# A rotation of 96 images by 90 degrees: the first group loaded in 8 KB rows and turned by way of PSUM, 1 MB of the last group stored in half rows

## The chip, the core and the metric

The kernel runs on one core of a Trainium2 chip. The metric is the device time of one execution in microseconds (us), lower is better; the time before is the median of three runs. Beside these, one execution was taken by the hardware profiler: its span (from the first to the last profiled instruction) and its own time are a little apart, and both are given below. The engines that matter here are VectorE (DVE in the profile), ScalarE (ACT), SyncE (SP), which issues all transfers, and the sixteen DMA engines that carry them between the device memory (HBM) and the on-chip memory (SBUF).

## The reference

```
x: (32, 3, 256, 256) float32
return np.rot90(x, k=-1, axes=(-2, -1)).astype(np.float32)
```

Every one of the 96 images of 256 x 256 is turned clockwise by a quarter: a transposition of each image, with the order of the new columns reversed. Nothing is computed; 25.17 MB are read and 25.17 MB are written.

## The kernel before

All 96 x 256 image rows are taken as one long list. A **slab** is 128 x 16 of them (2 MB): on each of the 128 partitions lie 16 rows of 256 floats, 16 KB. Four groups, u0 to u3, hold 2, 2, 4 and 4 slabs (4, 4, 8 and 8 MB, `sizes` at L38), all of them at once in SBUF, each with a buffer of its own. Two half-slab buffers `spare[0]` and `spare[1]` lie in PSUM, and `extra` and `most` in SBUF.

**Transfers.** SyncE issues every transfer, in the order of the program: first the loads of u0, u1, u2, u3 (L54 to L59), then the stores of u0 to u3 (L154 to L158). A load covers every second partition of u0 or u1 (64 partitions, rows of 16 KB) or every fourth of u2 or u3 (rows of 32 KB), 2 MB each; the very first and the very last load are cut into two of 1 MB. A store covers every second partition (64) with all slabs of the group, in rows of 16 KB: 2 MB for u0 and u1, 4 MB for u2 and u3, two stores a group (a = 0 and 1). The first store has a dependency by hand on `mark`, the first of the last two loads (L160), so that no store runs ahead of the loads. The transfers use eight semaphores in turn, so that a transfer also waits for the landing of the one eight places before it.

**The turn.** VectorE's transpose instruction turns blocks of 32 x 32; the rest of the rotation is done by the access patterns of its input (`src`, L83) and output (`dst`, L85), which permute positions inside a partition and reverse them. A group is turned in place. For this it is cut into quarters: by the halves of the input's column index c (low, high) and of its row index r, called A, B, C, D (L108). A quarter of a pair of slabs is 128 x 2048 elements. A quarter may overwrite only what has been read already, so one quarter first *leaves* into a spare buffer (L88, a VectorE turn into `spare` or `most`), the others *move* in place (L97), and the first *enters* by copies on ScalarE (L93). In u2 and u3, which have four slabs, some quarters are instead copied to a line buffer by ScalarE (`line`, L100), turned there by VectorE, and copied back (`unline`, L104).

**The order of the work.** `keep` (L63) chains all instructions of VectorE, and all of ScalarE, in the order in which they stand in the program. So the order around the change is written out by hand (L115 to L152): u0 leaves to `spare[0]`, moves D, C, B, and enters on ScalarE; u1 the same by way of `spare[1]`; then u2, whose first copy (`line` A into `extra`, L122) stands on ScalarE's queue ahead of the two copies that enter u1 (L124); then `line` D into `spare[1]` (L127); then the moves of u2. Of u3, a quarter of two slabs is first copied to `spare[1]` (`kept`, L136), a quarter leaves to `most` and a piece of `spare[0]`, six moves run (D, C, B, for each of two pairs of slabs), ScalarE's copies enter what left, and the last VectorE instruction turns `kept` into the last quarter (L152). That last turn writes the lower half of every 16 KB row of u3, and so do the copies before it; the upper halves are written by the moves of C and B.

Of the kernel before, what the change touches and what calls it, by code (L numbers as in the profile page):

```python
# [1 line left out]

# [4 lines left out]


@with_exitstack
def kernel(  # L10
    ctx: ExitStack,
    tc: tile.TileContext,
    x: bass.AP,
    out: bass.AP,
):

    nc = tc.nc
    fp32 = mybir.dt.float32

    B, C, H, W = x.shape
    P = nc.NUM_PARTITIONS
    R = 16
    E = R * W  # L30
    Q = E // 2
    hw = R // 2
    low, high = slice(0, hw), slice(hw, R)

    rows_in = x.rearrange("b c h w -> (b c h) w")
    rows_out = out.rearrange("b c h w -> (b c h) w")

    sizes = (2, 2, 4, 4)  # L38
    first = [sum(sizes[:n]) for n in range(len(sizes))]
    groups = [  # L40
        ctx.enter_context(tc.tile_pool(name=f"group{n}", bufs=1)).tile([P, s, E], fp32, name=f"u{n}")
        for n, s in enumerate(sizes)
    ]
    psum = ctx.enter_context(tc.tile_pool(name="psum", bufs=1, space=bass.MemoryType.PSUM))
    spare = [psum.tile([P, Q], fp32, name=f"spare{h}") for h in range(2)]
    extra = ctx.enter_context(tc.tile_pool(name="extra", bufs=1)).tile([P, Q], fp32, name="extra")
    cut = hw - 1
    most = ctx.enter_context(tc.tile_pool(name="most", bufs=1)).tile([P, Q // hw * cut], fp32, name="most")

    for n, I in enumerate(sizes):  # L50
        ld = rows_in[first[n] * P * R : (first[n] + I) * P * R]
        ld = ld.rearrange("(a i m r) w -> i m a (r w)", a=2, i=I, m=P // I)
        to = groups[n].rearrange("p s f -> p (s f)").rearrange("p (a f) -> p a f", a=2)
        for i in range(I):  # L54
            if (n, i) in ((0, 0), (len(sizes) - 1, I - 1)):
                mark = nc.sync.dma_start(out=to[i::I, 0], in_=ld[i][:, 0])  # L56
                nc.sync.dma_start(out=to[i::I, 1], in_=ld[i][:, 1])  # L57
            else:
                nc.sync.dma_start(out=to[i::I], in_=ld[i])  # L59

    last = {}

    def keep(inst):  # L63

        before = last.get(inst.ins.engine)
        if before is not None:
            tc.add_manual_dep(inst.ins, before, mybir.DependencyInfo(
                mybir.DependencyClass.NoSync, mybir.DependencyReason.SCHED_ONLY), reason="order")
        last[inst.ins.engine] = inst.ins.name

    def turn(out, in_):
        keep(nc.vector.transpose(out=out, in_=in_))  # L72

    def copy(out, in_):
        keep(nc.scalar.copy(out=out, in_=in_))  # L75

    class Group:
        def __init__(self, n):
            I = sizes[n]
            self.I, self.T = I, I // 2  # L80
            self.K = W // (R * self.T)
            u = groups[n].rearrange("p s f -> p (s f)")
            self.src = u.rearrange("p (a t r g c) -> p t c r g a", a=2, t=self.T, r=R, c=R)  # L83
            self.raw = u.rearrange("p (a t r g c) -> p t a r g c", a=2, t=self.T, r=R, c=R)
            self.dst = u.rearrange("p (i c k t r) -> p t c r k i", i=I, c=R, k=self.K, t=self.T)[:, ::-1, :, ::-1, ::-1, :]  # L85
            self.back = u.rearrange("p (i c k t r) -> p t i c k r", i=I, c=R, k=self.K, t=self.T)[:, ::-1]

        def leave(self, t, held, c=low, n=hw):  # L88

            kept = held.rearrange("p (i c k r) -> p c r k i", i=self.I, c=n, k=self.K)  # L90
            turn(out=kept[:, :, ::-1, ::-1, :], in_=self.src[:, t, c, low])

        def enter(self, t, held, i, c=low, n=hw):  # L93
            kept = held.rearrange("p (i c k r) -> p i c k r", i=self.I, c=n, k=self.K)
            copy(out=self.back[:, t, i, c, :, high], in_=kept[:, i])

        def move(self, t, c, r):  # L97
            turn(out=self.dst[:, t, c, r], in_=self.src[:, t, c, r])

        def line(self, t, c, r, row):  # L100
            row = row.rearrange("p (c r g a) -> p c r g a", c=hw, r=hw, a=2)
            copy(out=row, in_=self.src[:, t, c, r])

        def unline(self, t, c, r, row):  # L104
            row = row.rearrange("p (c r k i) -> p c r k i", c=hw, r=hw, k=self.K)
            copy(out=self.dst[:, t, c, r], in_=row)

    A, B_, C_, D = (low, low), (high, low), (high, high), (low, high)  # L108

    def turn_pair(g, held):  # L110
        g.leave(0, held)
        for q in (D, C_, B_):
            g.move(0, *q)

    g0, g1, g2, g3 = [Group(n) for n in range(4)]  # L115
    turn_pair(g0, spare[0])
    for i in range(2):
        g0.enter(0, spare[0], i)
    turn_pair(g1, spare[1])


    g2.line(0, *A, extra)  # L122
    g2.leave(1, spare[0])
    for i in range(2):  # L124
        g1.enter(0, spare[1], i)
    turn(out=extra, in_=extra)
    g2.line(0, *D, spare[1])  # L127
    g2.move(1, *D)
    turn(out=spare[1], in_=spare[1])
    g2.unline(0, *D, spare[1])  # L130
    for q in (C_, B_):
        for t in range(2):
            g2.move(t, *q)


    kept = spare[1].rearrange("p (a r g c) -> p a r g c", a=2, r=hw, c=hw)  # L136
    for a in range(2):
        copy(out=kept[:, a], in_=g3.raw[:, 0, a, low, :, low])
    for i in (0, 2, 1, 3):
        g2.enter(1, spare[0], i)  # L140
    rest = spare[0][:, : Q // hw]
    g3.leave(1, most, slice(0, cut), cut)
    g3.leave(1, rest, slice(cut, hw), 1)
    g2.unline(0, *A, extra)
    for q in (D, C_, B_):
        for t in range(2):
            g3.move(t, *q)
    for i in (0, 2, 1, 3):
        g3.enter(1, most, i, slice(0, cut), cut)
    held = rest.rearrange("p (i k r) -> p i k r", i=4, k=g3.K)  # L150
    copy(out=g3.back[:, 1, :, cut, :, high], in_=held)
    turn(out=g3.dst[:, 0, low, low], in_=kept.rearrange("p a r g c -> p c r g a"))  # L152

    for n, I in enumerate(sizes):  # L154
        st = rows_out[first[n] * P * R : (first[n] + I) * P * R]
        st = st.rearrange("(a i m r) w -> a m i (r w)", a=2, i=I, m=P // 2)
        for a in range(2):
            put = nc.sync.dma_start(out=st[a], in_=groups[n][a::2])  # L158
            if (n, a) == (0, 0):
                tc.add_manual_dep(put.ins, mark.ins.name, mybir.DependencyInfo(  # L160
                    mybir.DependencyClass.Sync, mybir.DependencyReason.SCHED_ONLY), reason="stores after loads")


# [1 line left out]
_INS = ['x']  # L165
_OUTS = [((32, 3, 256, 256), 'float32')]


# [23 lines left out]
```

## Time and profile before

| what | us |
|---|---|
| time, median of three runs (123.68 to 123.89) | 123.74 |
| the profiled execution's own time | 123.72 |
| its span | 121.9 |
| VectorE busy | 85.6 (25 turns) |
| ScalarE busy | 27.3 (20 instructions) |
| SyncE's queue: share of the sixteen DMA engines' span | 97.0% |
| first turn of u0 starts | 13.39 |
| first turn of u1 starts | 27.85 |
| first turn of u2 starts | 42.55 |
| first store issued | 59.61 |
| last turn ends | 99.52 |

The page gives the busy time of each engine, then the span in 40 equal slices with the busy share of a slice in tenths (9 is 90% or more), with the mean share of the DMA engines in the same slices; then the chain that ended last, and groups of instructions. In a line of a group or of the timeline stand the line of the kernel, the engine, the operation, output <- input by the program's names without buffer numbers (all four groups are `u` there), and what ended the engine's idle time before it. SPq is SyncE's queue, with the time that it spent on issuing a transfer, not the time of the transfer itself. Besides these views the trace holds, for each DMA packet, its start and length, and the moment of each landing.

### The profile page before, as it was taken

How to read it: one execution, taken by the hardware profiler on the slowest of the kernel's cores; microseconds unless marked ns; L12 is line 12 of the kernel's file. 1: busy time of each engine (PE TensorE's matmuls, PEld its weight loads, DVE VectorE, ACT ScalarE, POOL GpSimd, SP SyncE). 2: the span in 40 equal slices, each digit the busy share in tenths (PEclk: the TensorE clock that was granted, in tenths of full speed). 3: DMA queues.
4: the chain of work that ended last, by engine and by line, in shares of the span. 5: the costliest groups of instructions: out<-in, count | busy, mean ns of one | idle time of the engine just before them, and what ended most of it. 6: DMA issues, size and time to landing. Idle time of an engine off the chain costs nothing.

```text
span 121.9 us, 132 instructions
## 1 busy us (share of the span) xinstructions
DVE 85.6 (70%) x25; ACT 27.3 (22%) x20; POOL 0.2 (0%) x4
## 2 busy tenths in 40 slices
DVE  0000699999999999999999999999999960000000
ACT  0000400006000099928363194000003400000000
POOL 0000000000000000000000000000000000000000
DMA  3999999998979897979899999999999989999994
GB/s 86 387 430 435 441 435 435 446 505 355 516 344 516 344 516 344 516 344 516 344 430 430 430 430 430 425 425 430 430 430 430 430 355 430 430 430 430 430 430 172
DMA packets 2912, 50.33 MB, mean 413 GB/s; under 512 B 352, under 2 KB 352, under 8 KB 352
## 3 DMA queue, kind: packets, MB, share of 16 engines
q1 hardware_dynamic: 2912, 50.33, 97.0%
HBM read 25.17 MB, written 25.17 MB: 413 GB/s over the span
## 4 chain that ended last, share of the span: by engine, by line
DVE 44%; DMA 30%; SPq 4%; issue 3%; DVEq 0%
DVE u L72 33%; DMA u<-in_x_dram 30%; DVE spare L72 6%; SPq L59 3%; DVE most L72 3%; DVE extra L72 2%; SPq L56 0%; SPq L57 0%; DVEq L72 0%
## 5 line engine op out<-in xcount | busy, mean ns | idle before, releaser
L72 DVE STREAM_TRANSPOSE u<-u 128x2048 f32<-128x2048 f32 x17 | 62.6, 3734 | 0.3
L72 DVE STREAM_TRANSPOSE spare<-u 128x2048 f32<-128x2048 f32 (+1 forms) x4 | 11.9, 2979 | 13.6 <-DMA u<-in_x_dram 13.6
L75 ACT COPY u<-spare 128x1024 f32<-128x1024 f32 (+3 forms) x10 | 10.2, 1062 | 20.7 <-DVE u L72 18.0
L75 ACT COPY extra<-u 128x2048 f32<-128x2048 f32 x1 | 4.2, 4235 | 12.6 <-DMA u<-in_x_dram 12.6
L75 ACT COPY spare<-u 128x1024 f32<-128x1024 f32 (+1 forms) x3 | 6.0, 2016 | 2.9 <-DMA u<-in_x_dram 2.9
L75 ACT COPY u<-most 128x448 f32<-128x448 f32 x4 | 2.1, 564 | 20.3 <-DVE u L72 20.3
L75 ACT ACT_TABLE_LOAD x1 | 1.3, 1283 | 13.3 <-DMA u<-in_x_dram 13.3
L75 ACT COPY u<-extra 128x2048 f32<-128x2048 f32 x1 | 3.7, 3739 | 0.0
L72 DVE STREAM_TRANSPOSE u<-spare 128x2048 f32<-128x2048 f32 x1 | 3.6, 3605 | 0.0
L72 DVE STREAM_TRANSPOSE most<-u 128x1792 f32<-128x1792 f32 x1 | 3.6, 3603 | 0.0
L72 DVE STREAM_TRANSPOSE spare<-spare 128x2048 f32<-128x2048 f32 x1 | 2.5, 2474 | 0.0
L72 DVE STREAM_TRANSPOSE extra<-extra 128x2048 f32<-128x2048 f32 x1 | 2.3, 2311 | 0.0
L176 POOL MEMSET const-bfloat16-1.0<- 128x1 bf16 x1 | 0.1, 102 | 0.0
L176 POOL MEMSET const-uint8-127<- 128x1 uint8 x1 | 0.1, 102 | 0.0
L176 POOL MEMSET const-float32-1.0<- 128x1 f32 x1 | 0.1, 99 | 0.0
L176 POOL MEMSET const-float32-0.0<- 128x1 f32 x1 | 0.1, 98 | 0.2 <-issue 0.2
## 6 DMA issues: line engine op xcount, KB each, us to landing
u<-in_x_dram SPq DMA_DIRECT2D x10, 2048.0 KB, 30.2
out_dram<-u SPq DMA_DIRECT2D x4, 4096.0 KB, 18.7
out_dram<-u SPq DMA_DIRECT2D x4, 2048.0 KB, 13.4
u<-in_x_dram SPq DMA_DIRECT2D x4, 1024.0 KB, 20.5
```

What stands on the lines that cost most here:

```text
L59: nc.sync.dma_start(out=to[i::I], in_=ld[i])
L72: keep(nc.vector.transpose(out=out, in_=in_))
L75: keep(nc.scalar.copy(out=out, in_=in_))
L176: nc = _bacc.Bacc("TRN2", target_bir_lowering=False, num_devices=1)
```

## The change

For u0 the layout, the loads, the turn and the place in the program are new. A slab's 128 partitions now hold two runs of 8 rows from two places 1 MB apart, in rows of 8 KB. The second slab's rows come first, as two loads of 1 MB over all 128 partitions, then the first slab's as one load of 2 MB. The first slab buffer is turned by two VectorE instructions into `spare[0]` and `spare[1]`, the second one by two instructions into the first slab buffer, and ScalarE copies both spares into the second slab buffer in two copies of 128x2048. So the quarters, with `leave`, `move` and `enter`, are gone for u0; the number of VectorE instructions is the same. u1 leaves to `extra` instead of `spare[1]`, and it enters before u2's first copy and not after it. The stores of u0 keep their size and their 16 KB rows.

At the end, the store of the even partitions of u3 (a = 0, 4 MB) becomes three: the upper halves of slab 0's rows (64 x 8 KB, 512 KB), the lower halves (512 KB), and the other three slabs (3 MB). The a = 1 store stays whole.

```diff
-    for n, I in enumerate(sizes):
-        ld = rows_in[first[n] * P * R : (first[n] + I) * P * R]
-        ld = ld.rearrange("(a i m r) w -> i m a (r w)", a=2, i=I, m=P // I)
+    def rows_of(rows, n):
+        return rows[first[n] * P * R : (first[n] + sizes[n]) * P * R]
+    ld = rows_of(rows_in, 0).rearrange("(s i p r) w -> s i p (r w)", s=2, i=2, p=P)
+    home = [groups[0][:, s].rearrange("p (i f) -> p i f", i=2) for s in range(2)]
+    for i in range(2):
+        nc.sync.dma_start(out=home[0][:, i], in_=ld[1, i])
+    nc.sync.dma_start(out=home[1], in_=ld[0].transpose([1, 0, 2]))
+    for n in range(1, len(sizes)):
...
-    g0, g1, g2, g3 = [Group(n) for n in range(4)]
-    turn_pair(g0, spare[0])
+    def turn_slab(src, dsts):
+        s = src.rearrange("p (i r g c) -> p c r g i", i=2, r=R // 2, c=R)
+        for h, d in enumerate(dsts):
+            d = d.rearrange("p (c k r) -> p c r k", c=hw, r=R // 2)[:, :, ::-1, ::-1]
+            turn(out=d, in_=s[:, h * hw : (h + 1) * hw])
+    u = groups[0]
+    turn_slab(u[:, 0], spare)
+    turn_slab(u[:, 1], [u[:, 0, :Q], u[:, 0, Q:]])
+    for h in range(2):
+        copy(out=u[:, 1, h * Q : (h + 1) * Q], in_=spare[h])
+    g1, g2, g3 = [Group(n) for n in range(1, 4)]
+    turn_pair(g1, extra)
     for i in range(2):
-        g0.enter(0, spare[0], i)
-    turn_pair(g1, spare[1])
+        g1.enter(0, extra, i)
     g2.line(0, *A, extra)
     g2.leave(1, spare[0])
-    for i in range(2):
-        g1.enter(0, spare[1], i)
...
+    for n in range(1, len(sizes)):
+        I = sizes[n]
+        st = rows_of(rows_out, n).rearrange("(a i m r) w -> a m i (r w)", a=2, i=I, m=P // 2)
         for a in range(2):
-            put = nc.sync.dma_start(out=st[a], in_=groups[n][a::2])
+            done = 0
+            if (n, a) == (len(sizes) - 1, 0):
+                done = 1
+                for f in (slice(Q, E), slice(0, Q)):
+                    nc.sync.dma_start(out=st[a][:, 0, f], in_=groups[n][a::2, 0, f])
+            nc.sync.dma_start(out=st[a][:, done:], in_=groups[n][a::2, done:])
```

## The prediction

> **What bounds the kernel now.** I read the page's slices first, because they show how full the transfers are; then SyncE's own waits, since one queue issues every transfer; then the instructions in order of time around each border of the stages; last the transfer records, for the holes.
>
> The span and the slices of the page:
>
> ```profile
> span 121.9 us, 132 instructions
> ...
> DVE  0000699999999999999999999999999960000000
> ACT  0000400006000099928363194000003400000000
> ...
> DMA  3999999998979897979899999999999989999994
> ...
> DMA packets 2912, 50.33 MB, mean 413 GB/s; under 512 B 352, under 2 KB 352, under 8 KB 352
> ```
>
> The DMA row is at 9 nearly from end to end, while VectorE is idle in the first tenth and the last sixth. So the time is the start (first packet at 2.1 us), 50.33 MB at the engines' pace, whatever holes there are, and the end. The page's 97.0% for the queue leaves 3% of 121.9, about 3.7 us: 2.1 before the first packet, 1.3 after the last one at 120.65, and a remainder of some tenths.
>
> Where is the remainder? Windows of the trace (duration, then DVE, ACT and POOL busy, clock, DMA share, GB/s):
>
> ```profile
> 97.00:104.00 7.00, 2.52 (x1) 0.22 (x1) 0.00 (x0) 1.00 0.93 391
> 104.00:119.00 15.00, 0.00 (x0) 0.00 (x0) 0.00 (x0) 1.00 1.01 431
> ```
>
> A share of 0.93 over 7 us is 0.49 us missing. The transfer records place it: the sixteen engines run out between 100.29 and 100.74 and start again between 100.86 and 101.00, on average 0.44 us idle each. The instructions of that stretch say why:
>
> ```profile
> 92.17 1.04 ACT L75 COPY u<-most 128x448 f32<-128x448 f32 x2 [17.63 <-DVE u L72]
> 95.92 1.03 ACT L75 COPY u<-most 128x448 f32<-128x448 f32 x2 [2.71 <-DVE u L72]
> 95.92 3.60 DVE L72 STREAM_TRANSPOSE u<-spare 128x2048 f32<-128x2048 f32 x1
> 96.85 0.36 ACT L75 COPY u<-spare 128x256 f32<-128x256 f32 x1
> 99.60 1.26 SPq L158 DMA_DIRECT2D out_dram<-u  x2
> ```
>
> The last turn ends at 99.52, the stores of u3 are issued from 99.60, and their first packets come 1.27 us after that, at 100.87, when group 2's stores are already through. SyncE's waits from 95 us on confirm it:
>
> ```profile
> SPq L158 <- DVE u L72: 22.9, 1, 22.9
> SPq L187 <- DMA out_dram<-u: 20.1, 3, 10.2
> ```
>
> The two stores of u3 (4 MB each) land 10.19 and 9.74 us after what was before them; the 0.45 between is the hole. **So two things can change the time: how long the packets take, and that hole of 0.44 us.** VectorE matters through the hole alone.
>
> **Part 1: u0 in 8 KB rows, turned by way of PSUM.** The first turn of u0 now needs two loads of 1 MB instead of all 4 MB: by the landings of before (5.90, 8.36, 13.26) it starts 4.9 us earlier, at 8.4. Four turns at 3.60 to 3.63 remain four turns: two end at 15.6, two more at 22.9. u1 lands at 23.04 and its four turns end at about 37.6, against 42.38 before. But the next turn waits for u2, and before it also waited: ScalarE's and VectorE's first work on u2 starts at 42.49 and 42.55, released by the load. **The 4.9 us won at the start end in a wait of 4.9 us before u2.** What hides the edit is this slack. The two copies out of PSUM, 128x2048 each, at 3.88 (the copy u<-spare of that size) take 22.9 to 30.7 on ScalarE, beside u1's turns; they may slow these by the 0.62 that a turn shows beside a copy (4.22 at 42.55 against 3.60), at most 1.2 in all, within the slack. The new turn's shape is not in the trace: its nearest rows are 3.57 to 3.62 (to PSUM and to SBUF), and it costs nothing until four of them exceed the slack, 1.2 us each. u0's stores leave at 59.6 in any case, after the mark.
>
> What stays is packets: 4 MB in 8 KB rows is 512 instead of 256. Nothing in the trace has 8 KB rows. Nearest: loads of 2 MB land 4.88 and 4.90 us apart in 16 KB rows (u1), 4.85 to 4.87 in 32 KB rows (u2). That is 0.03 us for 64 packets more; 256 more: **+0.12 us**, between 0 and 0.25 (twice that). All later loads and landings shift with it.
>
> u1's copies (two of 1.0) move on ScalarE's queue from behind the first copy of u2 (46.63 to 48.53) to before it, so the copy D of u2 (4.01) starts at 46.7 instead of 48.56. Its overlap with u2's move of D (49.07 to 53.02, 3.95 from end to end against 3.6 alone) falls from 3.5 us to 1.7, which halves the 0.35 lost there: VectorE ends 0.15 us earlier against the transfers, between 0 and 0.3. The Trainium skill, *SBUF — State Buffer*, section "SBUF: two separate sides", says that of the engines' ports only the pair shared with GpSimd contends and that ScalarE and VectorE never wait on each other; by it this saving would be zero and the sum 0.15 higher. The 4.22 beside a copy against 3.60 without one speaks against the rule here, so I keep the row.
>
> **Part 2: the last group's half rows.** 1 MB of u3's first store becomes two of 512 KB, the other 3 MB a third. 64 packets more: +0.03; two more DMA instructions on SyncE at 0.60, issued while the queue holds work. The upper half does not depend on the last turn in its data: lower halves alone are written at 95.92 to 99.52. Issued at 95.95, it would fill the hole: -0.44, the most there is to win. But the built program says otherwise. **The first half-row store carries a wait for count 25 on VectorE's semaphore; the 24th is brought by the second move of B and the 25th by the last turn.** It is also behind the count of ScalarE's four copies out of `most`, done by 96.95. So it is issued where the whole store is issued now, at 99.5, and nothing leaves while the last quarter is turned. Queued behind it on SyncE are the lower half, the 3 MB and the last 4 MB, issued 0.65 us apart; 512 KB last 1.2 us (9.74/8), so each is there before the one ahead of it ends, and no second hole opens.
>
> The Trainium skill, *DMA: Bandwidth & Descriptors*, section "Bandwidth" with its rule of 1 MiB or more per DMA, speaks against this part: its fit of about 2.0 us plus bytes over 436 GB/s would charge some 4 us for two more transfers if each stood alone. In this trace the 2.0 is hidden wherever another transfer is queued: 1 MB loads land 2.45 us apart, which is bytes alone.
>
> What of the hole? VectorE's end against the transfers comes 0.15 earlier, so each engine's idle time falls by up to 0.15: 0.44 becomes 0.30, **-0.15**. With a saving of 0 it stays, with 0.3 it is 0.18 (the shortest holes close first).
>
> **Sum** against the profiled execution, 123.72 us (span 121.94 and 1.78 around it; the median of three is 123.74, 0.02 off): +0.12 packets of u0, +0.03 packets of u3, +0.02 for two more DMAs' own bookkeeping (0 to 0.05), -0.15 hole: +0.02, or 123.74. Ends: 123.72 - 0.26 = 123.46 with the packets free and the saving of 0.3, and 123.72 + 0.33 = 124.05 with the packets dear and no saving. I take **123.7**.
>
> **Rivals.**
> - *The hole closes* (the store of the upper half leaves before the last turn ends, or VectorE gains more than 0.45). For: the data are ready at 95.88. Against: the count it waits for. -0.44 + 0.17 = 123.45; with packets free, 123.28. Chance 0.25.
> - *Slower: the start is fed more slowly.* The first load (64 rows) reaches eight of the sixteen engines at 2.11 to 2.18 and the other eight at 2.75 to 2.85, 0.65 later. If that delay grows with the rows of a load, 128 rows make it 1.3, and half of the engines lose 0.65: 0.33 in the mean, and everything behind it, landings included, is late by that. With the +0.02: 124.05. It decides from about 0.25 of mean loss on. Against it: after the hole, a store of 256 packets reached all sixteen engines within 0.15 us. Chance 0.25, with what else is dear in small packets.
> - *It does nothing that can be measured*, which is the forecast: the part won on VectorE is waited away at 42.5, and the store that should fill the hole waits for the turn that makes it. Chance 0.5.
> - A new turn far slower than 4.8 us would break the slack and cost all that is over it; nothing in the rows suggests it, and it lies within the 0.25 of slower.
>
> **How the numbers follow.** About 0.2% (0.25 us) is what a measurement of this kernel can tell from no change: same is 123.49 to 123.99. Faster has 0.25, same 0.5, slower 0.25, and the predicted time is the likeliest case's. The range takes in both ends of the sum and both rivals: 123.3 to 124.15.
>
> **What would show it.** In the changed profile: u0's first turn starts near 8.4 us and VectorE waits about 4.9 us for u2 near 42.6; the copy D starts near 46.8; the first half-row store is issued after the last turn, near 99.5, and a window of 97 to 104 still misses 0.3 to 0.5 us of the DMA share. Wrong if that store is issued near 96, if u2 arrives later than 42.75, or if u0's turns run over 4.8 us.

## The result and the profile after

The changed kernel takes 123.29 us in the median of 15 runs, the kernel before 123.85 in 15 runs beside them: ratio 0.9961, interval 0.9947 to 0.9975. It is faster by 0.4% (0.25 to 0.53%). That is the lower edge of the range on record (123.3 to 124.15) and not the 123.7 that was forecast: the wait of the half-row stores was read rightly, but the start, which the sum took as fixed, moved, and the terms of the tail and of the hole were sized wrongly. The fifteen times are not one bunch: nine lie from 123.14 to 123.39 and six from 123.61 to 123.71. The profiled execution (123.70) belongs to the upper bunch, so its lines alone would show almost no gain.

The page of the changed kernel:

```profile
span 121.9 us, 135 instructions
...
DVE  0039999999994199999999999999999960000000
ACT  0000400470005199409462194000003400000000
...
DMA  3999999997979898989899999999999989999994
...
DMA packets 3264, 50.33 MB, mean 413 GB/s; under 512 B 384, under 2 KB 384, under 8 KB 384
```

VectorE's row starts two slices earlier and has a dent in the thirteenth and fourteenth slice: the time won at the start, waited away before u2. These are the first turn of u2, and the copy and the move of u2's quarter D, in the changed kernel and then before:

```profile
42.35 4.23 DVE L82 STREAM_TRANSPOSE spare<-u 128x2048 f32<-128x2048 f32 x1 [4.51 <-DMA u<-in_x_dram]
46.48 3.63 ACT L85 COPY spare<-u 128x2048 f32<-128x2048 f32 x1
48.84 3.86 DVE L82 STREAM_TRANSPOSE u<-u 128x2048 f32<-128x2048 f32 x1
```

```profile
42.55 4.22 DVE L72 STREAM_TRANSPOSE spare<-u 128x2048 f32<-128x2048 f32 x1 [0.17 <-DMA u<-in_x_dram]
48.56 4.01 ACT L75 COPY spare<-u 128x2048 f32<-128x2048 f32 x1
48.99 4.03 DVE L72 STREAM_TRANSPOSE u<-u 128x2048 f32<-128x2048 f32 x1
```

The turn of u2 has 4.51 us of idle time before it, released by the load, and the move of D takes 3.86 instead of 4.03: it now runs beside its copy for 1.3 us and not for 3.6. The end of the span, its instructions from 92 us on, the wait of SyncE there, and the two windows of the prediction:

```profile
88.62 7.37 DVE L82 STREAM_TRANSPOSE u<-u 128x2048 f32<-128x2048 f32 x2
92.28 1.03 ACT L85 COPY u<-most 128x448 f32<-128x448 f32 x2 [17.64 <-DVE u L82]
96.03 3.61 DVE L82 STREAM_TRANSPOSE u<-spare 128x2048 f32<-128x2048 f32 x1
96.03 1.03 ACT L85 COPY u<-most 128x448 f32<-128x448 f32 x2 [2.71 <-DVE u L82]
96.96 0.36 ACT L85 COPY u<-spare 128x256 f32<-128x256 f32 x1
99.71 1.13 SPq L189 DMA_DIRECT2D out_dram<-u  x2
100.89 1.99 SPq L190 DMA_DIRECT2D out_dram<-u  x2
```

```profile
SPq L189 <- DVE u L82: 22.9, 1, 22.9
SPq L216 <- DMA out_dram<-u: 18.0, 3, 9.7
```

```profile
97.00:104.00 7.00, 2.63 (x1) 0.33 (x2) 0.00 (x0) 1.00 0.87 365
104.00:119.00 15.00, 0.00 (x0) 0.00 (x0) 0.00 (x0) 1.00 1.03 437
```

Both half-row stores (L189) are issued after the last turn, from 99.71, as the count on VectorE's semaphore said: nothing leaves while the last quarter is turned. The hole is still there, and in this execution larger (a share of 0.87, against 0.93 before): 0.78 us in the mean of the sixteen engines by the transfer records, against 0.44.

**Where the time went.** While there is a hole, the end of a run is a plain sum: the last turn's end, the time to the first packets after it (mean of the sixteen engines), the packets of the last 8 MB, and what follows the last packet to the span's end. By the records of the profiled executions, in us:

| kernel | last turn ends | to the packets | packets of u3 | to the span's end | span |
|---|---|---|---|---|---|
| before | 99.52 | 1.39 | 19.74 | 1.29 | 121.94 |
| changed (upper bunch) | 99.63 | 1.28 | 19.84 | 1.17 | 121.92 |
| start_only, below | 99.16 | 1.39 | 19.75 | 1.29 | 121.58 |
| tail_slab, below | 99.62 | 1.28 | 19.76 | 1.22 | 121.88 |

So the change of the last store is worth -0.11 + 0.10 - 0.12, and the rest of the difference is when VectorE ends: 0.36 earlier than before, or 0.11 later. The experiments ask for each.

### The profile page after: what moved, and what is told of

It reads as the page before. It is cut to its first block, busy times and chain, and to the rows that moved or that the text cites. A ratio compares the mean times of both kernels' runs of the same rounds, so it can differ in the third digit from the quotient of the medians.

```text
span 121.9 us, 135 instructions
## 1 busy us (share of the span) xinstructions
DVE 86.6 (71%) x25; ACT 29.1 (24%) x20; POOL 0.2 (0%) x4
## 4 chain that ended last, share of the span: by engine, by line
DVE 44%; DMA 34%; issue 3%; DVEq 0%
DMA u<-in_x_dram 34%; DVE u L82 34%; DVE spare L82 6%; DVE most L82 3%; DVE extra L82 2%; DVEq L82 0%
## 5 line engine op out<-in xcount | busy, mean ns | idle before, releaser
L82 DVE STREAM_TRANSPOSE u<-u 128x2048 f32<-128x2048 f32 x16 | 59.7, 3811 | 0.3
L85 ACT COPY u<-spare 128x512 f32<-128x512 f32 (+2 forms) x8 | 10.5, 1347 | 18.6 <-DVE u L82 13.8
L85 ACT COPY u<-extra 128x1024 f32<-128x1024 f32 (+1 forms) x3 | 5.7, 1937 | 11.1 <-DVE u L82 11.1
L82 DVE STREAM_TRANSPOSE extra<-u 128x2048 f32<-128x2048 f32 x1 | 3.9, 3920 | 0.0
```

## The experiments

Times of before in the three groups of runs: 123.76, 123.72 and 123.75 us.

**The changed kernel again, and its two parts alone.** `start_only` leaves the last stores whole; `tail_only` puts the half-row stores into the kernel before.

```diff
# start_only, against the changed kernel
-            if (n, a) == (len(sizes) - 1, 0):
+            if False:
# tail_only, against the kernel before
+            if (n, a) == (len(sizes) - 1, 0):
+                done = 1
+                for f in (slice(Q, E), slice(0, Q)):
+                    nc.sync.dma_start(out=st[a][:, 0, f], in_=groups[n][a::2, 0, f])
```

> The changed kernel once more, beside its variants. Its fifteen times so far lie in two bunches, 123.1 to 123.4 and 123.6 to 123.7. Theory S (start): the gain is the first packet 0.31 us earlier, less 0.1 for smaller packets, and it is in both bunches; the bunches differ by when VectorE ends against the stores of group 2, that is by the hole (0.79 us on average in the profiled run of the upper bunch, about 0.3 in the lower one). Theory T (tail): the half rows bring the gain. Expected of both: median near 123.3; a profile of the lower bunch shows a hole near 0.3 and VectorE's last turn ending near 99.1.

> The changed kernel with the last stores whole as before: the first group's new loads and turns alone. Theory S: 123.25, as the changed kernel or up to 0.08 less, since the half rows bring nothing and cost the small packets. Theory T: 123.7 to 123.85, as before.

> The kernel before with the half-row stores alone. Theory S: 123.85 to 123.95, as before plus up to 0.08; the first half-row store is issued after the last turn, and the hole stays at 0.3 to 0.5. Theory T: 123.3.

Measured: changed 123.26 (ratio 0.9967, 0.9952 to 0.9983), again nine times from 123.06 to 123.41 and three from 123.68 to 123.80; its profile fell into the upper bunch once more (last turn ends at 99.66, hole 0.70). start_only 123.48 (0.9985, 0.9974 to 0.9997); tail_only 123.52 (0.9988, 0.9975 to 1.0001). Neither theory holds: by the medians each part brings about half, -0.28 and -0.24, and together they make -0.50. (The interval of tail_only just includes no gain; its repetition below does not.) The start is better than its sum said, and the half rows, though they wait, are not worthless.

**The half rows once more, and a cut without half rows.**

```diff
# tail_slab, in tail_only's place
-                for f in (slice(Q, E), slice(0, Q)):
-                    nc.sync.dma_start(out=st[a][:, 0, f], in_=groups[n][a::2, 0, f])
+                nc.sync.dma_start(out=st[a][:, 0], in_=groups[n][a::2, 0])
```

> The kernel before with the half-row stores alone, once more, for its interval. Theory I: 0.1 faster than before, 123.6 to 123.7. If the first measurement stands: 123.5.

> The kernel before with the first store of u3 cut into slab 0 (64 rows of 16 KB, 1 MB) and the other three slabs, no half rows. Theory I: what the half rows gained (0.24 in the median, with 1.0 at the edge of its interval) is that a smaller store is issued in less time, 0.50 against 0.60, and its packets come 0.1 sooner after the last turn; then this one, if its issue too takes 0.5, has a hole 0.1 smaller and is 0.1 to 0.2 faster than before, 123.55 to 123.65. If half rows themselves are what counts: 123.75.

Measured: tail_again 123.49 (0.9984, 0.9975 to 0.9993), tail_slab 123.59 (0.9991, 0.9979 to 1.0004; unclear by itself). The issue of u3's stores in tail_slab, and then in start_only, which stores whole (start, time spent on the issue, line, number):

```profile
99.69 0.49 SPq L161 DMA_DIRECT2D out_dram<-u  x1
100.23 1.97 SPq L162 DMA_DIRECT2D out_dram<-u  x2
```

```profile
99.23 1.26 SPq L190 DMA_DIRECT2D out_dram<-u  x2
```

SyncE spends 0.49 on issuing the small store (as for a half-row store), but 0.60 on the whole one (two in 1.26). The packets come 1.28 to 1.30 after the turn with a small first store, in the five profiles of this kind, and 1.39 with a whole one, in before and start_only: the 0.11 of the issue, whether its rows are half or whole. The other gain nobody had on the list: at the end SyncE tests the eight semaphores of the transfers in a fixed order, some 0.06 us a step. With 22 transfers the last store's semaphore is followed by two more steps (in before, records at 121.02, 121.08 and 121.14), with 24 by none: 1.29 falls to 1.17, and with 23 (tail_slab, one step) to 1.22. The half rows' packets cost 0.10 (19.84 against 19.74): in the changed kernel a stored packet of 8 KB takes 0.319 us and one of 16 KB 0.617, and each engine has eight of the small ones in place of four, which makes 0.08. By these terms the half rows are worth -0.13 and tail_slab -0.16. Measured were -0.24 and -0.26 (the second with an interval of -0.09 to -0.31) and -0.16. For the half rows a tenth is left within the interval, which is not explained.

**The store that really leaves early.** Here the wait of the upper halves for the last turn is taken away, by telling the scheduler that the two touch different bytes; it keeps the wait for the 24th count and for ScalarE's copies out of `most`.

```diff
...
-    turn(out=g3.dst[:, 0, low, low], in_=kept.rearrange("p a r g c -> p c r g a"))
+    final = turn(out=g3.dst[:, 0, low, low], in_=kept.rearrange("p a r g c -> p c r g a"))
...
-                    nc.sync.dma_start(out=st[a][:, 0, f], in_=groups[n][a::2, 0, f])
+                    half = nc.sync.dma_start(out=st[a][:, 0, f], in_=groups[n][a::2, 0, f])
+                    if f.start:
+                        tc.declare_no_dep(half.ins, final.ins, reason="upper half")
```

> The changed kernel, but the store of the upper halves is freed from the last turn: it waits for the 24th count of VectorE and not the 25th. If the hole is what the prediction said, the store is issued near 97.1, its packets follow group 2's without a gap, and the hole of 0.3 to 0.8 is gone: 122.8 to 123.0, with one bunch of times instead of two, because 1.2 us of packets cover either end of VectorE. If something else holds the stores back, 123.3.

> The freed store of the upper halves once more, for its interval: 122.9 to 123.1, no hole in the profile whatever the move of C takes.

Measured: 123.02 (0.9947, 0.9935 to 0.9960) and 122.92 (0.9935, 0.9921 to 0.9948). **This version beats both kernels**: by 0.74 and 0.80 against before, by 0.24 and some 0.34 against the changed one. (The interval of the first run overlaps that of the changed kernel, the interval of the repetition does not. The first run's six times spread from 122.80 to 123.30, so that they make one bunch is shown by the repetition alone, 122.88 to 123.04.) Its windows and its stores:

```profile
97.00:104.00 7.00, 2.66 (x1) 0.35 (x2) 0.00 (x0) 1.00 1.04 435
104.00:119.00 15.00, 0.00 (x0) 0.00 (x0) 0.00 (x0) 1.00 0.99 422
```

```profile
96.05 1.03 ACT L87 COPY u<-most 128x448 f32<-128x448 f32 x2 [2.71 <-DVE u L82]
96.05 3.61 DVE L82 STREAM_TRANSPOSE u<-spare 128x2048 f32<-128x2048 f32 x1
96.99 0.37 ACT L87 COPY u<-spare 128x256 f32<-128x256 f32 x1
97.11 3.11 SPq L191 DMA_DIRECT2D out_dram<-u  x2
```

The line of L191 merges both half-row stores; the first is issued at 97.11, when ScalarE's copies out of `most` are done (97.08) and while the last quarter is turned, and the hole is gone (0.00 in the records). VectorE ended at 99.66 in the first of these profiles and at 99.16 in the second, and both executions took 123.02: without the hole its end no longer counts. The difference to the changed kernel's profiled run, 0.68, is its hole of 0.78 within 0.1.

**Why two bunches.** In the changed kernel the first move of C (VectorE, in place) starts 0.12 us before ScalarE's copy of D out of `spare[1]` and runs beside it. The pair, first in the changed kernel, then in start_only:

```profile
54.80 4.30 DVE L82 STREAM_TRANSPOSE u<-u 128x2048 f32<-128x2048 f32 x1
54.92 4.31 ACT L85 COPY u<-spare 128x2048 f32<-128x2048 f32 x1 [4.82 <-DVE spare L82]
```

```profile
54.78 3.84 DVE L82 STREAM_TRANSPOSE u<-u 128x2048 f32<-128x2048 f32 x1
54.92 3.84 ACT L85 COPY u<-spare 128x2048 f32<-128x2048 f32 x1 [4.80 <-DVE spare L82]
```

The same two instructions at nearly the same distance, 4.30 or 3.84 each. The two profiles of the early version, which are of one and the same kernel, show it too: 4.30 in the one whose last turn ends at 99.66, 3.83 in the one where it ends at 99.16. To see what the copy costs, it is left out (one quarter of u2 is then not written):

```diff
-    g2.unline(0, *D, spare[1])
```

> The changed kernel without ScalarE's copy of quarter D out of spare[1] into u2 (128x2048): that quarter of u2 is not written. Theory C (contention): in the profiles that end late this copy and VectorE's first move of C run beside each other in 4.31 and 4.30 us, in the one that ends early in 3.84 and 3.84; without the copy the move takes 3.6 to 3.7, VectorE ends at 99.0 or earlier, the hole is 0.2 or less, and the times lie in one bunch at 123.0 to 123.15. Without C: two bunches as in the changed kernel, median 123.25.

Measured: 122.98 (0.9936, 0.9924 to 0.9949), in five runs from 122.75 to 123.05: one bunch.

```profile
54.66 3.56 DVE L82 STREAM_TRANSPOSE u<-u 128x2048 f32<-128x2048 f32 x1
```

The move takes 3.56, the last turn ends at 98.59, and the hole is 0.02. So the copy costs this move 0.3 to 0.7 us. The one bunch proves less than was expected of it, because without a hole VectorE's end does not count, as in the early version. That the bunches of the changed kernel are the two speeds of this pair rests on the sizes: 4.30 - 3.84 = 0.46, and the bunches' middles are 123.24 and 123.67. Both profiles of that kernel fell into the upper bunch (4.30 and 4.29), so its lower bunch was not seen directly. Why the pair runs at one speed or the other is not settled; in the kernel before and its variants it took 3.87 to 4.17. The Trainium skill, *SBUF — State Buffer*, section "Who interferes with whom", has it that only the port pair of VectorE and GpSimd makes engines wait; by it this copy could cost nothing, and 3.56, 3.84 and 4.30 speak against it.

**What makes the start faster.** In the changed kernel the first packet came at 1.80, before at 2.11. Is it the length of the rows, or the number of partitions in a load? `first_half` cuts the first load of before into two of 64 rows of 8 KB. `early_4k` cuts the first load of the early version into two of 4 KB rows on 128 partitions. `early_even` keeps bytes, rows and number of loads of the early version, but gives each of the first two loads every second partition, and `early_block` the lower and the upper 64.

```diff
# first_half, against the kernel before
-                mark = nc.sync.dma_start(out=to[i::I, 0], in_=ld[i][:, 0])
+                parts = (slice(0, Q), slice(Q, E)) if n == 0 else (slice(None),)
+                for f in parts:
+                    mark = nc.sync.dma_start(out=to[i::I, 0][:, f], in_=ld[i][:, 0][:, f])
# early_4k, against the early version
+    for f in (slice(0, Q // 2), slice(Q // 2, Q)):
+        nc.sync.dma_start(out=home[0][:, 0, f], in_=ld[1, 0][:, f])
+    nc.sync.dma_start(out=home[0][:, 1], in_=ld[1, 1])
# early_even, against the early version; early_block has (slice(0, P // 2), slice(P // 2, P))
+    for h in (slice(0, P, 2), slice(1, P, 2)):
+        nc.sync.dma_start(out=home[0][h], in_=ld[1].transpose([1, 0, 2])[h])
```

> The kernel before with its first load (64 rows of 16 KB) cut into two loads of 64 rows of 8 KB. It asks what makes the first packet of the changed kernel come at 1.75 to 1.80 us and not at 2.11: there SyncE spent 0.38 us on issuing the first load and not 0.60, and the packet followed the end of the issue by 0.64 to 0.78 in all runs. Theory R (the length of a row): the issue takes 0.40 or less, the first packet is at 1.8 or earlier, u2 lands 0.2 earlier. Theory P (64 rows on every second partition are slower to issue than 128 rows on all): the issue takes 0.49 to 0.60 and the first packet is at 2.0 to 2.1; then u2 lands within 0.1 of before. Time: 123.5 by R, 123.7 by P.

> The freed store, and the first load cut into two of 512 KB in 4 KB rows over all 128 partitions. If the first packet follows the end of the issue and the issue follows the bytes of a row, the first packet comes at 1.7 or earlier and the time falls by up to 0.1 against the freed store alone, less 0.05 for 128 packets more. If the issue does not depend on the bytes, the same as the freed store or 0.05 more.

> The kernel with the freed store (122.92 to 123.02), and the first two loads of 1 MB each over 64 partitions (every second one, two rows of 8 KB each) instead of over all 128: the same bytes, rows and number of loads. Theory P, that a load of all 128 partitions is issued faster: SyncE takes 0.5 to 0.6 us for the first load, its first packet is at 2.0 to 2.1 and u2 lands 0.2 later than with all partitions: 123.15 to 123.25. If partitions do not matter: issue 0.38 to 0.40, first packet 1.75 to 1.80, 122.95.

> The same with the lower 64 partitions in the first load and the upper 64 in the second. If the step of two partitions makes the issue slow, this one is as fast as all 128 (first packet 1.8, 122.95); if the number of partitions does, it is like the load of every second one (first packet 2.0 to 2.1, 123.2).

Measured: first_half 124.99 (1.0099, 1.0085 to 1.0113), early_4k 123.84 (1.0009, 1.0001 to 1.0018), early_even 123.37 (0.9966, 0.9954 to 0.9978), early_block 127.87 (1.0332, 1.0319 to 1.0345). SyncE's first issues before, in the changed kernel, in first_half and in early_even:

```profile
0.73 0.60 SPq L56 DMA_DIRECT2D u<-in_x_dram  x1
1.39 0.57 SPq L57 DMA_DIRECT2D u<-in_x_dram  x1
```

```profile
0.73 0.85 SPq L58 DMA_DIRECT2D u<-in_x_dram  x2
```

```profile
0.74 1.23 SPq L58 DMA_DIRECT2D u<-in_x_dram  x2
```

```profile
0.73 1.43 SPq L58 DMA_DIRECT2D u<-in_x_dram  x2
```

The numbers are the start and the time spent on the issue, or on both where the line has x2. Two loads of 128 partitions are issued in 0.85 us, two of 64 in 1.23 or 1.43, and the first packet comes at 1.80, 2.15 and 2.24. The length of the row is not it: 64 rows of 8 KB take 0.60 like 64 rows of 16 KB, and 128 rows of 4 KB 0.38 like 128 rows of 8 KB. In early_even u2 lands at 42.65, in the early version at 42.25, and the time is 0.35 to 0.45 longer. So the start's gain hangs on first loads that cover all 128 partitions. early_block's first issue takes as long as early_even's (0.75 and 0.74), so it is the number and not the step.

Two misses teach more. In first_half and early_4k the time rose by far more than a packet's price. In first_half the third load lands at 9.63, where the same bytes land at 8.36 before, and u2 at 43.74 instead of 42.47: from 5.3 to 6.1 us up to four of the sixteen engines stood idle (0.14 us in the mean of all, 0.05 before), and the 16 KB packets up to that landing took 0.71 us in the mean instead of 0.61. By their number (102) that is 0.6 us an engine, so some 0.7 of the 1.27 is accounted for and the rest is not. In early_4k the first two loads of 512 KB take 1.68 us from one landing to the next, in place of 1.2. Whether the 512 KB of the first load or the small rows are to blame was not separated; 8 KB rows in first loads of 1 MB did not have it (changed kernel, early_even). And early_block moved 223 GB/s from 3 to 8 us, the early version 429:

```profile
3.00:8.00 5.00, 0.00 (x0) 0.00 (x0) 0.00 (x0) 1.00 0.99 223
```

The engines are busy (0.99), but packets of 8 KB take 0.64 instead of 0.31 us. The Trainium skill, *SBUF — State Buffer*, section "Door 1: The DMA port swizzle", says that bit 6 of a partition's number chooses between two halves of the ports, so that 64 neighbouring partitions reach only half of them; this run agrees with it.

## Why the prediction was half right, step by step

- **u0's slack: right.** VectorE had its wait of 4.5 us before u2 (forecast 4.9); the first turn started at 8.19 (8.4). The new turn took 3.56 to 4.01, far from what would break the slack. The two copies out of PSUM took 1.87 each and not the 3.88 of the nearest row, but nothing waited for them.
- **Packets of u0, +0.12: the term was right and the step wrong.** From the first landing to u0's last one it is 7.46 us against 7.36, so the small packets cost 0.10. But u2 landed 0.20 earlier (42.27 against 42.47), not 0.12 later: the step took the first packet's time as fixed. It came 0.31 earlier: 0.22 because the issue of the first load took 0.38 and not 0.60, and 0.09 because the packet followed the end of the issue sooner. The gain at u2's landing is not the same in every execution: 0.20 and 0.09 in the two profiles of the changed kernel, 0.22 in start_only. The rival of a slower start had the wrong sign; the trace of before has issue times for loads of 64 and 32 partitions alone, so the price of 128 was unknown, and its bounds should have reached below nothing.
- **VectorE 0.15 earlier after u2: right in the speed of the lower bunch.** The move of D lost 0.17 (4.03 to 3.86). From u2's first turn to the last turn's end it is 56.97 us before and 56.83 in start_only. In the upper bunch it is 57.28: the pair of 4.30 that the prediction did not price (it had 4.02 beside 3.88 in before and took that as fixed).
- **The hole, 0.44 to 0.30: wrong.** In start_only it is 0.43: VectorE ends 0.36 earlier, but the transfers of group 2 run out earlier too (100.12 against 100.47 in the mean), since their first packet came 0.35 earlier. In the two profiles of the changed kernel it grew to 0.78 and 0.70.
- **The half rows wait for the 25th count: right**, and with it that nothing leaves during the last turn. Freed from it, the store closes the hole, as the first rival had it; the early version is 0.74 to 0.80 faster than before.
- **Two more DMAs, +0.02: wrong sign.** A shorter issue (-0.11) and two steps fewer in the last test of semaphores (-0.12). The packets of u3 cost 0.10 where 0.03 was put. The fit of 2.0 us a transfer that the prediction set against this part stands on its page in the section "Anatomy of one DMA — SWDGE (gpsimd) path", for transfers that GpSimd issues; here SyncE issues all of them, and behind a filled queue the small ones cost no more than this 0.10.
- **Sum.** For the lower bunch, 123.72 - 0.36 (VectorE's end, as in start_only: u2's landing 0.22, the saving 0.14) - 0.11 + 0.10 - 0.12 = 123.23, measured 123.14 to 123.39. For the upper, 123.72 + 0.11 - 0.13 = 123.70, measured 123.61 to 123.71. The upper bunch's sum uses the lines of that bunch's own profile, so it only shows that the terms are complete. The forecast of 123.74 was the upper bunch's time by luck: it left out a gain at the start and a loss at the pair. The favoured case, a change too small to measure (123.49 to 123.99, chance 0.5), did not come; "faster" (0.25) did, but not by the way it was given, a hole that closes.

## What to carry to other kernels

- A store that is cut off so that it may leave early leaves early only if its wait says so: read the count that it waits for, and if it names an instruction that doesn't write its bytes, free it. Here that was worth half as much again as the whole change.
- Where a stream of transfers runs dry for one late engine, the time is that engine's end plus a fixed tail; a gain ahead of it counts only as far as it moves that end, and the first transfer of the tail should be the one that is quickest to issue.
- One profile of a kernel whose times lie in two bunches shows one of them: look at the single times before reading a difference out of it.

## What the runs showed of the hardware that was not expected

The issue of a first load took 0.38 to 0.40 us for 128 partitions and 0.60 to 0.75 for 64, and the first packet followed its end by 0.63 to 0.95 us. A move on VectorE beside a ScalarE copy ran at 3.84 or at 4.30 us, the same instructions at nearly the same distance, and in 3.56 without the copy. Loads of 64 neighbouring partitions ran at 223 GB/s, loads of every second partition at 413 (from 3 to 8 us). The two kernels whose first load was cut to 512 KB were 0.8 to 1.3 us slower than without that cut; the cause was not separated.
